# A two-layer mLSTM block and a sparse-attention block on one core: the reciprocal-root chains at the changes of stage, with one SBUF tensor per instruction

## The chip, the cores and the metric

The kernel runs on one core of a Trainium2 chip. The metric is the time of one execution on the device in microseconds (us). Five engines work side by side, each through its own list of instructions in order: TensorE (PE, matmuls and transposes), VectorE (DVE), ScalarE (ACT), GpSimd (POOL) and SyncE (SP, which only issues transfers here). They wait for each other through semaphores. SBUF is the large on-chip memory, PSUM the small one into which TensorE writes its results (the kernel's pool divides it into eight banks).

## The reference, cut to what matters

512 tokens of width 1024 pass through two layers of a first block and one layer of a second. Each layer of the first block is

```python
h = rms_norm(x, g_pre_mix) * (1 + sc_mix) + sh_mix
y = mixer(h, ...)                                   # mLSTM heads and a convolution branch, then @ w_out
x = x + gt_mix * rms_norm(y, g_post_mix)
h = rms_norm(x, g_pre_mlp) * (1 + sc_mlp) + sh_mlp
f = jnp.square(jax.nn.relu(h @ w_ff1)) @ w_ff2
x = x + gt_mlp * rms_norm(f, g_post_mlp)
```

with `rms_norm(x, g) = x * lax.rsqrt(mean(x*x) + 1e-6) * g` per token. The second block has attention, a feed-forward part of the same kind and a last rms_norm. So between two large products there is always this: a sum of squares per token, a reciprocal root, `x` updated, again a sum of squares, again a reciprocal root, and the normed tokens are what the next product reads.

## The kernel before, in words

Every matrix product is done in three matmuls on halves of fp32 numbers (`mm3`, L202 to L204: high by high, high by low, low by high). Weights come as 128x1024 tiles `wr` on SyncE's queue; `prep` makes the high half `w` on ACT (L178) and the low half either on POOL in four pieces of 128x256 (L182) or on DVE in one piece (L69). Which engine it is, is set per chunk of weights by the tuple `pool` of the stage's table `TUNE`. All DVE work that goes through the wrapper `Paced` has line L69, the line of the wrapper, whatever it does; such instructions are told apart by their tiles: `c` are the tiny columns (128x1, 128x2 or 128x4), `E` the token tiles (128x1024), `hT` the transposed and split activations, `t` scratch, `p` PSUM banks.

A change of stage is the place where one product's output, token by token, becomes the next product's input. There are six: after the mixer of layer 0 (near 430 us), after its feed-forward part (near 810), after the mixer of layer 1 (near 1195), after its feed-forward part (near 1575), inside the second block (near 1965), and the last norm at the end. The first four go through `post_norm`. There a tile of 128 tokens is `y[i]`, four tiles in all. When the second half of a tile's product is complete, `ready` lets ACT sum its squares (tile `j`, L580) and POOL multiply it by the gate row (L582). `update` then runs, for a pair of tiles (`w` = 2; first, third and fourth change) or for a single tile (`w` = 1; second change, where `TUNE` has pt=1):

- `s1`, the sum of the two half sums (DVE);
- a reciprocal-root chain `rsqrt` on the 128xw column: a guess from the bits and two polynomial steps, each instruction reading the one before it (DVE, 9 instructions for w > 1, 7 for w = 1);
- `x += r * y` per tile (DVE, tile `E<-E,c,E`, 128x1024), its squares summed on ACT (L593), and a store;
- `norm_T`: a second chain of the same kind, then `x` scaled by its result into `to`. For a pair ACT does both halves of the first tile (L460) and DVE both halves of the second.

After that `norm_T2` transposes on TensorE (L475, 16 transposes of 128x128 for a pair, eight column blocks of two tiles), ACT and DVE bring them out with scale and shift (`t`), ACT writes the high half and DVE the low half of `hT`, and the next product (`p<-hT,w`) can begin with these two tiles while the other two are still on their way.

The order of instructions on each engine is not the order of the source. A scheduler of the tile layer places them by priorities and its own cost estimates. `self.soon()` raises the priority of the norm by `TUNE`'s `bp` (1000, 1000, 200 and 0 in the four changes of stage), `work_off` says where in the stream of matmuls the transposes are emitted. So an edit of the chain's instructions can move others.

The functions of the diff and their callers follow, with the profile's line numbers.

Of the kernel before, what the change touches and what calls it, by code (L numbers as in the profile page):

```python
# [10 lines left out]
I32 = mybir.dt.int32  # L11
AFTER = mybir.DependencyInfo(mybir.DependencyClass.NoSync, mybir.DependencyReason.DATA)
AF = mybir.ActivationFunctionType
OP = mybir.AluOpType

T, D, DFF = 512, 1024, 4096
NL, NH, DH = 2, 4, 256
KC, KM = 31, 4
EPS = 1e-6
# [27 lines left out]
RSQRT_C, RSQRT_GUESS = 1.5 ** 0.2, 0x5f05a21f  # L47
# [25 lines left out]
class Kern:  # L73
    def __init__(self, ctx, tc, A, out, dump=None, stop=None):
        self.tc, self.nc, self.A, self.out = tc, tc.nc, A, out
        self.V = Paced(self, tc.nc.vector)
        self.pt = self.dt = 0.0
# [96 lines left out]
    def prep(self, i):  # L174
        raw, w = self.units[i], self.plan[i][1]
        u = self.units[i] = self.tile("w", (128, 2, 1024), F32R)
        with self.later("prep"):
# [5 lines left out]
            else:  # L183
                self.V.tensor_tensor(u[:, 1, :w], raw[:, :w], f32(u[:, 0, :w]), op=OP.subtract)
        self.prepped += 1
# [36 lines left out]
            nc.scalar.activation(hi, src, AF.Copy if isinstance(scale, float) else AF.Identity, scale=scale)  # L222
            self.V.scalar_tensor_tensor(lo, src, scale, f32(hi), op0=OP.mult, op1=OP.subtract)

    def rsqrt(self, src, w, mul, add, tag=None):

        V = self.V
        vh, z, q, y1, y = (self.c(w, tag) for _ in range(5))

        def half_square(z):  # L230
            a = self.c(w, tag)
            if w == 1:
                V.scalar_tensor_tensor(a, z, vh, z, op0=OP.mult, op1=OP.mult)
            else:
                V.tensor_tensor(a, z, z, op=OP.mult)
                V.tensor_tensor(a, a, vh, op=OP.mult)
            return a
        V.tensor_scalar(vh, src, 0.5 * mul, 0.5 * add, op0=OP.mult, op1=OP.add)
        V.tensor_scalar(z.bitcast(I32), vh.bitcast(I32), -0.5, RSQRT_GUESS, op0=OP.mult, op1=OP.add)
        h = half_square(z)  # L240
        V.scalar_tensor_tensor(q, h, -RSQRT_C ** 2 * 5 / 3, h, op0=OP.add, op1=OP.mult)
        V.scalar_tensor_tensor(y1, q, RSQRT_C ** 4 * 5 / 4, z, op0=OP.add, op1=OP.mult)
        a = half_square(y1)
        V.scalar_tensor_tensor(y, a, 1.5, y1, op0=OP.subtract, op1=OP.mult, reverse0=True)
        return y
# [199 lines left out]
        for ev, b in zip(evacs, bs):  # L445
            ev(b)

    def norm_T(self, ii, xs, ss, G, sh, to):

        V, w = self.V, len(xs)  # L450
        if ii == 0:
            self.new_hT()
        r = self.rsqrt(ss, w, 1.0 / D, EPS)
        for b in range(2):
            h = slice(512 * b, 512 * b + 512)
            for t in range(w):
                if (t if w > 1 else b):
                    V.tensor_scalar(to[t][:, h], xs[t][:, h], r[:, t:t + 1], None, op0=OP.mult)
                else:
                    self.nc.scalar.activation(to[t][:, h], xs[t][:, h], AF.Copy, scale=r[:, t:t + 1])  # L460
        self.xn += to
        if len(self.xn) == 2:
            i, x, self.xn = ii + w - 2, self.xn, []
            for q in range(4):
                self.pend.append((i, lambda q=q: self.norm_T2(i, q, x, G, sh)))
# [92 lines left out]
    def post_norm(self, l, which, nxt):  # L558

        nc, V = self.nc, self.V  # L560
        self.ada_wait(l, range(16 + 24 * which, 24 + 24 * which))
        row = self.gate_row(l, which)
        GS = nxt()
        self.n += 1
        dst = self.dram.tile([T, D], F32, name=f"xd{self.n}")
        src = self.xsrc
        self.xsrc = [dst[i * 128:(i + 1) * 128, :] for i in range(4)]
        xs, ss, w = [None] * 4, {}, 1 if self.tune["pt"] else 2

        def ready(i, nh):  # L570
            y, t = self.y[i], i % w
            self.calm = nh == 1 and CALM
            h = slice(nh * 512, (nh + 1) * 512)
            if nh == 0:
                xs[i] = self.tile("E", (128, D))
                nc.sync.dma_start(xs[i], src[i])
                if t == 0:
                    ss[i // w] = self.c(2 * w)
            with self.soon():
                nc.scalar.activation(self.tile("j", (128, 512), BF16), y[:, h], AF.Square,  # L580
                                     accum_out=ss[i // w][:, w * nh + t:w * nh + t + 1])
                nc.gpsimd.tensor_tensor(y[:, h], y[:, h], row[:, h], op=OP.mult)  # L582
            return (lambda: update(i - t)) if nh and t == w - 1 else None

        def update(i):
            with self.soon():
                s, s1, s2 = ss[i // w], self.c(w), self.c(w)
                V.tensor_tensor(s1, s[:, 0:w], s[:, w:2 * w], op=OP.add)
                r = self.rsqrt(s1, w, 1.0 / D, EPS)
                for t in range(w):  # L590
                    n, x = i + t, xs[i + t]
                    V.scalar_tensor_tensor(x, self.y[n], r[:, t:t + 1], x, op0=OP.mult, op1=OP.add)
                    nc.scalar.activation(self.y[n].bitcast(BF16)[:, 0:D], x, AF.Square, accum_out=s2[:, t:t + 1])  # L593
                    nc.sync.dma_start(self.xsrc[n], x)
                    self.dbg(f"x{l}{which}_{n}", x)
                self.norm_T(i, xs[i:i + w], s2, *GS, self.y[i:i + w])
        return ready


# [1059 lines left out]
```

## Time and profile before

| | |
|---|---|
| median of 3 runs | 2338.77 us (2337.93 to 2339.65) |
| the profiled execution's own time | 2338.5 us |
| its span in the trace | 2336.8 us |
| TensorE busy | 2224.5 us, 95% of the span |
| VectorE / ScalarE / GpSimd busy | 1484.2 / 972.6 / 709.3 us (64% / 42% / 30%) |
| chain that ended last, by engine | PE 75%, DVE 14%, ACT 4%, issue 2%, POOL 2%, DMA 1% |
| mean granted TensorE clock | 0.982 of full speed |

The profile covers one execution. Of TensorE it says that it is nearly always busy; the rest of the span, 112 us, is spread over many short waits. The profile's own time lies 1.7 us above the span, and that part is taken as constant. The chain of work that ended last is followed back from the last instruction, so a share of DVE in it is time in which TensorE had to wait for work on DVE, or in which DVE alone was left at the end.

### The profile page before, as it was taken

The numbers are of one execution on the slowest core, as the hardware profiler recorded it, in microseconds if no ns is written. First come the engines' busy times: TensorE is split into PE (matmuls) and PEld (weight loads), VectorE is DVE, ScalarE is ACT, GpSimd is POOL, SyncE is SP. The second block draws the span as 40 slices with busy tenths as digits, with TensorE's granted clock in tenths as the row PEclk, the third lists the DMA queues.
The fourth block names the chain that finished last, engine by engine and source line by source line (L and its number), as shares of the span: only waits on it lengthen the run. The fifth ranks groups of instructions, "written<-read, shape, count | busy, mean of one in ns | idle before, by whom it ended". The sixth has DMA issues, their size and how long they took to land.

```text
span 2336.8 us, 28930 instructions
## 1 busy us (share of the span) xinstructions
PE 2224.5 (95%) x10552; PEld 1811.9 (78%) x10552; DVE 1484.2 (64%) x2927; ACT 972.6 (42%) x1697; POOL 709.3 (30%) x934
## 2 busy tenths in 40 slices
PE   5998999799999999999989999998989999999998
PEld 3777887688888777788768888877878888888886
DVE  6698998645677669999663233346996435443434
ACT  3435554433232354555443323234447544332322
POOL 4645561425335254565341201212212330000000
PEclk9999999899999999999999999999999999999999
DMA  7524236336666433222333423323111234322232
GB/s 281 166 83 136 64 92 214 109 127 213 211 207 207 145 100 89 74 69 68 114 107 90 135 90 99 99 81 114 55 55 55 64 108 153 104 95 95 88 105 82
DMA packets 77758, 271.37 MB, mean 116 GB/s; under 512 B 9008, under 2 KB 9776, under 8 KB 77616
## 3 DMA queue, kind: packets, MB, share of 16 engines
q1 hardware_dynamic: 69840, 241.21, 32.1%
q0 software_dynamic: 7776, 28.32, 3.8%
q8 instruction: 83, 1.36, 0.2%
q14 instruction: 59, 0.48, 0.1%
HBM read 256.91 MB, written 12.58 MB: 115 GB/s over the span
## 4 chain that ended last, share of the span: by engine, by line
PE 75%; DVE 14%; ACT 4%; issue 2%; POOL 2%; DMA 1%; SPq 0%; ACTq 0%; DVEq 0%; POOLq 0%
PE p L202 23%; PE p L204 23%; PE p L203 23%; DVE p L839 3%; DVE c L69 3%; DVE E L69 1%; POOL w L182 1%; PE p L475 1%; DMA ad<-in_ada_dram 1%; DVE w L69 1%; DVE s L69 1%; ACT w L178 1%; PE p L621 1%; PE p L1211 1%; DVE hT L69 1%
## 5 line engine op out<-in xcount | busy, mean ns | idle before, releaser
L182 POOL TENSOR_TENSOR w<-wr,w 128x256 fp32r<-128x256 f32 x648 | 493.5, 794 | 722.1 <-ACT w L178 629.4
L178 ACT ACTIVATE w<-wr 128x1024 fp32r<-128x1024 f32 (+1 forms) x353 | 369.2, 1048 | 598.1 <-PE p L204 523.1
L202 PE MATMUL p<-hT,w 128*128 128x512 f32 (+1 forms) x1504 | 577.1, 385 | 15.4 <-ACT hT L214 7.3
L203 PE MATMUL p<-hT,w 128*128 128x512 f32 (+1 forms) x1504 | 573.0, 381 | 9.4 <-POOL hT L218 5.4
L204 PE MATMUL p<-hT,w 128*128 128x512 f32 (+1 forms) x1504 | 573.4, 382 | 1.5 <-POOL w L182 1.5
L202 PE MATMUL p<-w,s 128*128 128x512 f32 (+1 forms) x1152 | 450.8, 391 | 3.5 <-ACT s L214 3.5
L204 PE MATMUL p<-w,s 128*128 128x512 f32 (+1 forms) x1152 | 448.8, 390 | 0.6 <-DVE s L69 0.6
L203 PE MATMUL p<-w,s 128*128 128x512 f32 (+1 forms) x1152 | 448.5, 389 | 0.6 <-DVE w L69 0.6
L69 DVE TENSOR_TENSOR w<-wr,w 128x1024 fp32r<-128x1024 f32 (+1 forms) x187 | 233.0, 1247 | 290.9 <-ACT w L178 290.5
L202 PEld LDWEIGHTS p<-hT,w 128*128 128x128 f32 x1504 | 286.2, 191 | 74.7 <-ACT hT L214 9.6
L839 DVE SCALAR_TENSOR_TENSOR p<-ga,ad,p 128x495 f32<-128x495 f32 (+24 forms) x480 | 339.3, 728 | 6.6 <-ACT p L834 5.5
L203 PEld LDWEIGHTS p<-hT,w 128*128 128x128 f32 x1504 | 286.3, 190 | 67.3 <-POOL hT L218 6.5
L204 PEld LDWEIGHTS p<-hT,w 128*128 128x128 f32 x1504 | 286.1, 190 | 57.8 <-POOL w L182 3.8
L202 PEld LDWEIGHTS p<-w,s 128*128 128x128 f32 x1152 | 217.1, 188 | 52.1 <-ACT s L214 4.5
L204 PEld LDWEIGHTS p<-w,s 128*128 128x128 f32 x1152 | 217.0, 188 | 50.1 <-DVE s L69 1.5
L203 PEld LDWEIGHTS p<-w,s 128*128 128x128 f32 x1152 | 217.3, 189 | 49.3 <-DVE w L69 1.0
L69 DVE TENSOR_TENSOR E<-p,E 128x512 f32<-128x512 f32 (+4 forms) x152 | 94.8, 638 | 145.7 <-PE p L204 117.5
L69 DVE SCALAR_TENSOR_TENSOR t<-p,t 128x512 f32<-128x512 f32 x96 | 65.9, 687 | 127.8 <-ACT t L1033 127.8
L296 DVE SCALAR_TENSOR_TENSOR ad<-ad,ad 128x1024 f32<-128x1024 f32 x80 | 107.2, 1345 | 53.6 <-DMA ad<-in_ada_dram 53.6
L1033 ACT ACTIVATE t<-p 128x512 f32<-128x512 f32 x96 | 56.7, 590 | 163.7 <-PE p L204 163.7
L69 DVE TENSOR_TENSOR s<-t,s 128x512 fp32r<-128x512 f32 (+1 forms) x100 | 102.1, 1021 | 12.8 <-ACT s L1035 7.3
L582 POOL TENSOR_TENSOR E<-E,s 128x512 f32<-128x512 f32 x32 | 45.9, 1441 | 168.7 <-ACT j L580 168.7
(272 smaller groups left out, 2648.7 us busy)
## 6 DMA issues: line engine op xcount, KB each, us to landing
wr<-in_ff_dram SPq DMA_DIRECT2D x128, 512.0 KB, 3.8
wr<-in_win_dram SPq DMA_DIRECT2D x64, 512.0 KB, 3.8
ad<-in_ada_dram POOLq DMA_DIRECT2D x54, 512.0 KB, 4.8
wr<-in_wout_dram SPq DMA_DIRECT2D x40, 512.0 KB, 3.8
wr<-in_up_dram SPq DMA_DIRECT2D x32, 512.0 KB, 3.6
wr<-in_down_dram SPq DMA_DIRECT2D x32, 512.0 KB, 3.5
ad<-in_ada_dram SPq DMA_DIRECT2D x26, 512.0 KB, 4.6
xd<-E SPq DMA_DIRECT2D x20, 512.0 KB, 2.7
```

The costliest lines, as they stand in the source:

```text
L69: return f(out, *a, **kw)
L178: self.nc.scalar.activation(u[:, 0, :w], raw[:, :w], AF.Copy)
L182: self.nc.gpsimd.tensor_tensor(u[:, 1, o:e], raw[:, o:e], f32(u[:, 0, o:e]), op=OP.subtract)
L202: mm(out, lh, rh, start=first, stop=False)
L203: mm(out, lh, rl, start=False, stop=False)
L204: self.mm = mm(out, ll, rh, start=False, stop=last)
L296: return self.nc.vector.scalar_tensor_tensor(w, w, 1.0, self.cact, op0=OP.mult, op1=OP.mult, accum_out=m)
L475: nc.tensor.transpose(p[:, k, 128 * t:128 * t + 128], x[t][:, j * 128:(j + 1) * 128], self.ident)
L582: nc.gpsimd.tensor_tensor(y[:, h], y[:, h], row[:, h], op=OP.mult)
L621: nc.tensor.matmul(p[32 * h:32 * h + 32, (c // 2) * 256:(c // 2) * 256 + 256], wg[:, h, c, e, :], ws[3 * h + c][:, e, :], start=c != 1 and ...
L839: V.scalar_tensor_tensor(y[:, d:], a[:, :T - d], w[:, o - d:o - d + 1], y[:, d:], op0=OP.mult, op1=OP.add)
L1033: nc.scalar.activation(r, p, AF.Relu)
```

## The change

`rsqrt` gets two new forms beside the old one, which stays for 128x4 columns and for the pair chains outside `post_norm`.

- For w = 1, wherever it is called, every instruction becomes a `tensor_scalar`: one tensor, and the other factors as per-partition scalars (pointers to a 128x1 column). There are 7 instructions as before. It serves the second change of stage (eight chains) and the last norm (four chains). `s1` becomes a `tensor_scalar` too.
- For w = 2 with `new` given, three of the intermediate values (`z`, `hp`, `y1`) are written to slots of one PSUM bank (tag `pc`), so that every instruction has at most one tensor in SBUF among its inputs. The square by half is computed as `a = vh*z`, then twice `a*z`, once into PSUM and once into SBUF, since the next step wants both; the chain has 10 instructions in place of 9. It serves the first, third and fourth change of stage (four chains each). The first step, `vh`, still reads SBUF and writes SBUF. The `s1` of a pair still reads two SBUF columns.

```diff
--- before.py
+++ after.py
@@ -222,18 +222,41 @@
             nc.scalar.activation(hi, src, AF.Copy if isinstance(scale, float) else AF.Identity, scale=scale)
             self.V.scalar_tensor_tensor(lo, src, scale, f32(hi), op0=OP.mult, op1=OP.subtract)
 
-    def rsqrt(self, src, w, mul, add, tag=None):
+    def rsqrt(self, src, w, mul, add, tag=None, new=None):
 
         V = self.V
+        if w == 1:
+            vh, z, h, q, y1, a, y = (self.c(w, tag) for _ in range(7))
+            ts = V.tensor_scalar
+            ts(vh, src, -0.5 * mul, -0.5 * add, op0=OP.mult, op1=OP.add)
+            ts(z.bitcast(I32), vh.bitcast(I32), -0.5, RSQRT_GUESS - 2 ** 30, op0=OP.mult, op1=OP.add)
+            ts(h, z, vh, z, op0=OP.mult, op1=OP.mult)
+            ts(q, h, RSQRT_C ** 2 * 5 / 3, h, op0=OP.add, op1=OP.mult)
+            ts(y1, q, RSQRT_C ** 4 * 5 / 4, z, op0=OP.add, op1=OP.mult)
+            ts(a, y1, vh, y1, op0=OP.mult, op1=OP.mult)
+            ts(y, a, 1.5, y1, op0=OP.add, op1=OP.mult)
+            return y
+        if new:
+            vh, a, h, q, b, c, y = (self.c(w, tag) for _ in range(7))
+            z, hp, y1 = (new() for _ in range(3))
+            tt, stt = V.tensor_tensor, V.scalar_tensor_tensor
+            V.tensor_scalar(vh, src, 0.5 * mul, 0.5 * add, op0=OP.mult, op1=OP.add)
+            V.tensor_scalar(z.bitcast(I32), vh.bitcast(I32), -0.5, RSQRT_GUESS, op0=OP.mult, op1=OP.add)
+            tt(a, vh, z, op=OP.mult)
+            tt(hp, a, z, op=OP.mult)
+            tt(h, a, z, op=OP.mult)
+            stt(q, hp, -RSQRT_C ** 2 * 5 / 3, h, op0=OP.add, op1=OP.mult)
+            stt(y1, q, RSQRT_C ** 4 * 5 / 4, z, op0=OP.add, op1=OP.mult)
+            tt(b, vh, y1, op=OP.mult)
+            tt(c, b, y1, op=OP.mult)
+            stt(y, c, 1.5, y1, op0=OP.subtract, op1=OP.mult, reverse0=True)
+            return y
         vh, z, q, y1, y = (self.c(w, tag) for _ in range(5))
 
         def half_square(z):
             a = self.c(w, tag)
-            if w == 1:
-                V.scalar_tensor_tensor(a, z, vh, z, op0=OP.mult, op1=OP.mult)
-            else:
-                V.tensor_tensor(a, z, z, op=OP.mult)
-                V.tensor_tensor(a, a, vh, op=OP.mult)
+            V.tensor_tensor(a, z, z, op=OP.mult)
+            V.tensor_tensor(a, a, vh, op=OP.mult)
             return a
         V.tensor_scalar(vh, src, 0.5 * mul, 0.5 * add, op0=OP.mult, op1=OP.add)
         V.tensor_scalar(z.bitcast(I32), vh.bitcast(I32), -0.5, RSQRT_GUESS, op0=OP.mult, op1=OP.add)
@@ -445,12 +468,12 @@
         for ev, b in zip(evacs, bs):
             ev(b)
 
-    def norm_T(self, ii, xs, ss, G, sh, to):
+    def norm_T(self, ii, xs, ss, G, sh, to, new=None):
 
         V, w = self.V, len(xs)
         if ii == 0:
             self.new_hT()
-        r = self.rsqrt(ss, w, 1.0 / D, EPS)
+        r = self.rsqrt(ss, w, 1.0 / D, EPS, new=new)
         for b in range(2):
             h = slice(512 * b, 512 * b + 512)
             for t in range(w):
@@ -566,6 +589,13 @@
         src = self.xsrc
         self.xsrc = [dst[i * 128:(i + 1) * 128, :] for i in range(4)]
         xs, ss, w = [None] * 4, {}, 1 if self.tune["pt"] else 2
+        scr = []
+
+        def new():
+            if not scr:
+                p = self.bank((128, 64, 8), "pc")
+                scr.extend(p[:, i, 0:w] for i in range(64))
+            return scr.pop()
 
         def ready(i, nh):
             y, t = self.y[i], i % w
@@ -585,15 +615,18 @@
         def update(i):
             with self.soon():
                 s, s1, s2 = ss[i // w], self.c(w), self.c(w)
-                V.tensor_tensor(s1, s[:, 0:w], s[:, w:2 * w], op=OP.add)
-                r = self.rsqrt(s1, w, 1.0 / D, EPS)
+                if w == 1:
+                    V.tensor_scalar(s1, s[:, 0:1], s[:, 1:2], None, op0=OP.add)
+                else:
+                    V.tensor_tensor(s1, s[:, 0:w], s[:, w:2 * w], op=OP.add)
+                r = self.rsqrt(s1, w, 1.0 / D, EPS, new=new)
                 for t in range(w):
                     n, x = i + t, xs[i + t]
                     V.scalar_tensor_tensor(x, self.y[n], r[:, t:t + 1], x, op0=OP.mult, op1=OP.add)
                     nc.scalar.activation(self.y[n].bitcast(BF16)[:, 0:D], x, AF.Square, accum_out=s2[:, t:t + 1])
                     nc.sync.dma_start(self.xsrc[n], x)
                     self.dbg(f"x{l}{which}_{n}", x)
-                self.norm_T(i, xs[i:i + w], s2, *GS, self.y[i:i + w])
+                self.norm_T(i, xs[i:i + w], s2, *GS, self.y[i:i + w], new)
         return ready
```

The scheduler places other instructions differently for this. On TensorE at the first change of stage (line L475 is L498 now; p729 is the accumulator of the last token tile, E579 and E580 are the first pair's normed tiles, hT what the next product reads) the program before has

```order
L204 MATMUL p729_3956<-w730_3957,s714_3897 128x512
L475 MATMUL p759_4135<-identr_82,E579_3181 128x128
...
L475 MATMUL p766_4175<-identr_82,E580_3182 128x128
L202 MATMUL p729_3956<-w730_3957,s715_3903 128x512
L203 MATMUL p729_3956<-w730_3957,s715_3903 128x512
L204 MATMUL p729_3956<-w730_3957,s715_3903 128x512
L202 MATMUL p790_4254<-hT749_4067,w732_3962 128x256
```

and the changed one, in the same place,

```order
L204 MATMUL p729_3956<-w730_3957,s714_3897 128x512
L202 MATMUL p729_3956<-w730_3957,s715_3903 128x512
L203 MATMUL p729_3956<-w730_3957,s715_3903 128x512
L204 MATMUL p729_3956<-w730_3957,s715_3903 128x512
L498 MATMUL p760_4138<-identr_82,E579_3181 128x128
...
L498 MATMUL p767_4178<-identr_82,E580_3182 128x128
L202 MATMUL p791_4259<-hT750_4069,w732_3962 128x256
```

The last three matmuls of the old product stood behind the 16 transposes and now stand ahead of them; it is the same at the third change of stage and at the fourth, where the three had stood between the transposes. At the second, ten matmuls instead of six stand ahead of the first large group of transposes, which are now 12 in a row, and 22 instead of 11 ahead of the last tile's. On VectorE at the fourth change of stage (the first pair's second chain, then what follows; w are weights split for the next product, E1988 or E1990 the evacuation of the last token tile, E1986 or E1988 the DVE half of the pair's normed tiles) the program before has

```order
L69 SCALAR_TENSOR_TENSOR c2259_13344<-c2262_13349 128x2
L69 SCALAR_TENSOR_TENSOR c2260_13345<-c2259_13344,c2258_13343 128x2
L69 TENSOR_TENSOR c2263_13354<-c2260_13345 128x2
L69 TENSOR_TENSOR c2263_13354<-c2263_13354,c2257_13342 128x2
L69 SCALAR_TENSOR_TENSOR c2261_13346<-c2263_13354,c2260_13345 128x2
L69 TENSOR_SCALAR E1986_11402<-E2225_13193,c2261_13346 128x512
L69 TENSOR_TENSOR w2238_13244<-wr2221_13159,w2238_13244 128x1024
L69 TENSOR_TENSOR w2240_13249<-wr2237_13242,w2240_13249 128x1024
...
L69 TENSOR_TENSOR E1988_11404<-p2235_13238,E1988_11404 128x512
```

and the changed one

```order
L69 TENSOR_TENSOR c2262_13356<-c2261_13355,p2257_13335 128x2
L69 TENSOR_TENSOR w2240_13254<-wr2223_13169,w2240_13254 128x1024
L69 TENSOR_TENSOR w2242_13259<-wr2239_13252,w2242_13259 128x1024
L69 SCALAR_TENSOR_TENSOR c2263_13357<-p2257_13335,c2262_13356 128x2
L69 TENSOR_TENSOR E1990_11414<-p2237_13248,E1990_11414 128x512
L69 SCALAR_TENSOR_TENSOR p2257_13335<-c2263_13357,p2257_13335 128x2
L69 TENSOR_TENSOR c2264_13358<-c2260_13354,p2257_13335 128x2
L69 TENSOR_TENSOR c2265_13359<-c2264_13358,p2257_13335 128x2
L69 SCALAR_TENSOR_TENSOR c2266_13360<-c2265_13359,p2257_13335 128x2
...
L69 TENSOR_SCALAR E1988_11412<-E2227_13203,c2266_13360 128x512 x2
```

Two weight splits and the evacuation of the last tile have moved from behind the chain into its middle, and the normed halves come after them all. On ScalarE there the second pair's last sum of squares also moved ahead of the first pair's scaling. On TensorE there the second pair's transposes stand 4 matmuls earlier in the next product than before (after 44 instead of 48, with the remaining ones between and behind them).

## Rows read from the trace of the kernel before

**Rows 1.** The page, part 1: busy us, share of the span, instructions.

```profile
PE 2224.5 (95%) x10552; PEld 1811.9 (78%) x10552; DVE 1484.2 (64%) x2927; ACT 972.6 (42%) x1697; POOL 709.3 (30%) x934
```

**Rows 2.** Waits of TensorE: engine line, releaser: us in total, times, longest.

```profile
PE p L475 <- ACT E L460: 21.7, 7, 4.4
```

**Rows 3.** Timeline of TensorE: start us, us, what; in brackets idle before it, releaser.

```profile
434.87 3.68 PE L475 MATMUL p<-identr,E 128*128 128x128 f32 x16 [3.38 <-ACT E L460]
438.20 0.78 PE L202 MATMUL p<-w,s 128*128 128x512 f32 x1
...
440.24 0.69 PE L202 MATMUL p<-hT,w 128*128 128x256 f32 x2 [0.41 <-ACT hT L214]
...
456.00 0.47 PE L475 MATMUL p<-identr,E 128*128 128x128 f32 x1 [4.42 <-ACT E L460]
...
1221.01 0.47 PE L475 MATMUL p<-identr,E 128*128 128x128 f32 x1 [4.41 <-ACT E L460]
```

**Rows 4.** Timeline of VectorE at the first change of stage.

```profile
429.31 0.38 DVE L69 TENSOR_SCALAR c<-c 128x2 f32<-128x2 f32 x2 [0.62 <-ACT E L593]
...
430.11 1.16 DVE L69 SCALAR_TENSOR_TENSOR c<-c 128x2 f32<-128x2 f32 x1
...
434.03 1.79 DVE L69 TENSOR_SCALAR E<-E,c 128x512 f32<-128x512 f32 x2
...
441.67 1.25 DVE L69 TENSOR_TENSOR c<-c 128x2 f32<-128x2 f32 x1
...
449.32 2.85 DVE L69 SCALAR_TENSOR_TENSOR E<-E,c,E 128x1024 f32<-128x1024 f32 x2
```

**Rows 5.** Timeline of GpSimd, and one row of ScalarE, at the same place.

```profile
429.96 1.29 POOL L582 TENSOR_TENSOR E<-E,s 128x512 f32<-128x512 f32 x1 [6.05 <-ACT j L580]
431.22 5.88 POOL L182 TENSOR_TENSOR w<-wr,w 128x256 fp32r<-128x256 f32 x8
429.79 1.99 ACT L178 ACTIVATE w<-wr 128x1024 fp32r<-128x1024 f32 x2
```

**Rows 6.** Windows: PE, PEld, DVE, ACT, POOL busy (x), PEclk, DMA share, GB/s.

```profile
434.80:438.60 3.80, 3.73 (x17) 3.73 (x18) 2.24 (x5) 1.67 (x5) 2.29 (x3) 0.50 0.59 155
1576.00:1579.40 3.40, 2.89 (x19) 2.21 (x19) 3.40 (x5) 1.85 (x5) 0.00 (x0) 1.00 0.39 95
```

**Rows 7.** VectorE: groups by form, a line's durations (min/median/max), unhindered pair chain.

```profile
L69 DVE TENSOR_SCALAR c<-c 128x1 f32<-128x1 f32 x12 | 1.8, 152 | 4.5 <-ACT E L593 4.4
...
L69 DVE TENSOR_SCALAR c<-c 128x2 f32<-128x2 f32 x1 | 1.2, 1166 | 0.0
...
L839 DVE SCALAR_TENSOR_TENSOR p<-ga,ad,p x480: 691/728/756, 72.5 to 1137.0; 128x508 f32<-128x508 f32 x12, 128x505 f32<-128x505 f32 x11, 128x493 f32<-128x493 f32 x11, 128x490 f32<-128x490 f32 x11
...
1957.99 0.16 DVE L69 TENSOR_TENSOR c<-c 128x2 f32<-128x2 f32 x1 [0.85 <-ACT j L1440]
...
1959.96 0.89 DVE L69 TENSOR_SCALAR ad<-E,c 128x512 f32<-128x512 f32 x2
```

**Rows 8.** Timeline of TensorE and VectorE at the second change of stage.

```profile
812.15 0.33 PE L475 MATMUL p<-identr,E 128*128 128x128 f32 x1 [3.15 <-DVE c L69]
...
832.96 0.33 PE L475 MATMUL p<-identr,E 128*128 128x128 f32 x1 [2.22 <-ACT E L460]
...
808.65 2.49 DVE L69 SCALAR_TENSOR_TENSOR c<-c,c 128x1 f32<-128x1 f32 x3
```

**Rows 9.** Timeline of TensorE and VectorE at the fourth change of stage.

```profile
1576.07 0.33 PE L475 MATMUL p<-identr,E 128*128 128x128 f32 x1 [1.46 <-ACT E L460]
...
1593.75 0.33 PE L475 MATMUL p<-identr,E 128*128 128x128 f32 x1 [2.40 <-ACT E L460]
...
1575.63 2.35 DVE L69 TENSOR_TENSOR w<-wr,w 128x1024 fp32r<-128x1024 f32 x2
...
1581.30 1.28 DVE L69 TENSOR_TENSOR c<-c 128x2 f32<-128x2 f32 x1
```

**Rows 10.** Timeline of VectorE at the last norm (its third step, one pointer scalar).

```profile
2330.72 0.22 DVE L69 SCALAR_TENSOR_TENSOR c<-c,c 128x1 f32<-128x1 f32 x1
```

## The prediction

> **What bounds the kernel now.** I read the page's busy shares first, then TensorE's waits, then the timeline at each change of stage. TensorE is busy for 95% of the span [rows 1], so a shorter instruction elsewhere gains only where TensorE stands and waits for it. The list of waits names such a place: the transposes L475 wait for ScalarE's scaling L460 seven times, 21.7 us in all [rows 2]. At the first change of stage these are 3.38 us before the first pair's transposes and 4.42 us before the second's; the third change repeats them (its 4.41 stands in [rows 3]). ScalarE itself waits there for VectorE's second chain.
>
> Why is that chain late? VectorE starts it at 429.31 and scales with its result at 434.03 [rows 4]: 4.72 us. The same chain with its first sum takes 1957.99 to 1959.96, 1.97 us, inside the second block [rows 7], so one tiny instruction costs 0.2 us. The difference is GpSimd. At 430.11 an instruction on two numbers lasts 1.16 us [rows 4], and it ends with GpSimd's 1.29 us instruction of 429.96; then eight GpSimd pieces run to 437.10 [rows 5] and each chain step takes about one of them. In the same way the second pair's first chain (with the hT conversions between its steps) goes from 441.67 to 449.32 [rows 4].
>
> Which instructions are held? Those with two tensors in SBUF. The convolution taps L839 read one from SBUF and one from PSUM and write PSUM: 480 of them, between 691 and 756 ns [rows 7], never held, although GpSimd works through that stretch. The 128x1 `tensor_scalar` has a mean of 152 ns [rows 7], not held either. These are the two forms that the change uses.
>
> **The pair form, step by step (first and third change).** Ten instructions instead of nine: +0.2 us per chain. That PSUM as output or input costs nothing extra is an assumption; the taps' 756 ns for about 500 elements leaves room for some 0.06 us an instruction, so a chain costs between +0.2 and +0.8 us where nothing held it.
>
> - `vh`, the first step, still reads and writes SBUF. It took 1166 ns once [rows 7], so it stays held where GpSimd is at work when it comes, and I count no gain for it. The Trainium skill says ("SBUF — State Buffer", Who interferes with whom) that a `tensor_scalar` whose tensor and output are both in SBUF may use both ports and then contends with GpSimd as well; the trace agrees with its 1166 ns.
> - First pair. The update chain gets 0.2 us longer. The second chain starts at 429.5, before GpSimd does, and ends at 431.5 in place of 434.03. Now ScalarE is next: two weight conversions keep it until 431.78 [rows 5], 432.0 with the shift. The transposes start 0.84 us behind the chain today [rows 3, 4], so at 432.8 instead of 434.87: 2.1 us.
> - The three matmuls that today follow the transposes run ahead of them and end near 432.2. TensorE's wait shrinks from 3.38 to about 0.6 us. Behind 3.38 us of waiting its granted clock was 0.50, the 1.2 GHz level; behind 1.46 us it was 1.00, 2.4 GHz [rows 6, 9]. So I expect full clock: 16 transposes in 1.9 us instead of 3.68, and the three matmuls, the first of which takes 0.78 us today [rows 3], at full clock too. The next product's first matmul, 5.4 us behind the first transpose today [rows 3], comes some 3.5 us behind, at 436.3 instead of 440.24.
> - Second pair. Its last product is evacuated before, not behind, the first pair's transposes: its `s1` moves from 441.67 to about 435.2. From there today's 7.65 us [rows 4] become about 6.4, shorter by one hold like that of `s1` (1.25 us); the other holds, on the conversions, stay. The two updates start at 441.6 instead of 449.32. Behind them the same work as today, 0.2 us for the tenth step and up to 0.6 us more of holds, since GpSimd's next pieces now fall on them: transposes at 449.1 instead of 456.00, 6.9 us. Is TensorE there by then? Today it takes 11.3 us from 440.24 to the start of its wait, 4.42 us before 456.00; from 436.3 that is 447.6, so the chain still ends last and the 6.9 us count.
>
> First change: -6.9. Third change, the same rows 766 us later and the same moves in the order: -6.9. Bounds for each: -3 (the first pair's gain without clock and move, and 1 us of the second's) and -9 (the second wait also falls so low that the clock stays up).
>
> **The single-tile form (second change).** Seven instructions stay seven, but five have pointer scalars. One pointer made 0.22 us of 0.16 [rows 10]; three steps more have one, and `s1`: +0.25 us per chain. Against that three steps of 2.49 us [rows 8] become about 0.65 in the second tile's second chain, which TensorE waits for 3.15 us [rows 8]. With the hold on the scaling half that is left, the transposes start at about 809.9 instead of 812.15, and four more matmuls (0.9 us at the mean of 0.21 us each, 2224.5 over 10552 [rows 1]) are done by then; the wait falls to about 1 us and the half clock behind it goes (1.2 us). Less 0.5 us for a conversion that TensorE then has to wait for (0.41 in the first change [rows 3]): -4. The last tile's transposes wait 2.22 us today [rows 8]. Eleven more matmuls of half the width now stand ahead of them (1.2 us) and its chain comes 4 to 5 us earlier, so most of that wait and part of the slow clock behind it go: -3. Sum -7; bounds -2 (weights or loads take over) and -9.
>
> **The fourth change** goes the other way. There GpSimd splits no weights, so little is held; instead the scheduler has put two weight splits, 2.35 us together [rows 9], and the last evacuation into the middle of the first pair's second chain, and the scaling comes behind. Then GpSimd's next gate product falls on the scaling as it falls today on `s1`, for 1.28 us [rows 9]. The transposes come at about 1579.6 instead of 1576.07, TensorE waits some 4.3 instead of 1.46 us, and behind such a wait it has run at half clock [rows 3, 6]. The second pair's update starts 1.4 us later; its transposes, today at 1593.75 after 2.40 us of waiting [rows 9], come near 1595.3, but TensorE reaches them only at about 1596.4, with four matmuls still to do. Against today +2.3; bounds 0 and +5.
>
> **The last norm** lies on the path: four pointer steps of 0.06 us, +0.25. The kernel's other chains (128x4 columns, the second block's pair) are unchanged.
>
> **Sum.** -6.9 - 6.9 - 7.0 + 2.3 + 0.25 = -18.2 us. Made against the profiled execution, 2338.5 us, that is 2320.3; the median of the runs is 0.3 us higher. I predict 2321. A measurement of this kernel tells about 0.2% from no change, 4.7 us.
>
> **Rivals.**
>
> - *The next wait takes over.* Each product behind a change needs its weights split in time, and ScalarE and GpSimd work through these splits in the same microseconds [rows 5]. If the second pair still meets its weights or its holds on the four conversions (two SBUF tensors, unchanged), only the first pair's 2 us and 1 to 2 us of clock come through per change: -3 to -4 three times, +2.3 and +0.3, about -8: 2330. For it: all engines are dense there. Against it: no wait for weights is near the length of those on L460.
> - *Reading PSUM is slow.* By this each instruction with PSUM among its inputs is later by some 0.06 us, nothing in a matmul's scale but eight times in a chain, with three chains on the path in each of three changes: about +5, so 2326. Against it: the taps' 691 to 756 ns, PSUM on both sides with a pointer. The Trainium skill gives this rule ("VectorE: DVE Perf Modes", The TRN2 errata): a fixed 120 cycles for PSUM to SBUF against 58 within SBUF. By that figure, an estimate, it is 65 ns an instruction, and the sum would be the same 2326.
> - *The holds do not go.* If an instruction waited for GpSimd whatever it reads, the longer pair chains would pay one more hold of about 0.7 us and only the moved matmuls would gain: within 4 us of before. Against it: 480 taps.
> - *Slower.* The moved weight splits of the fourth change decide: 3.5 us later transposes, half clock over the 40 matmuls behind them as well (4 us at most), and the second pair's wait pushed out with them: +8 there, while the others give -1 each: 2344. It decides from the point where TensorE has no full clock until the second pair's transposes. For it: the order shows the move. Against it: only one of four changes has it, and a wait there of 1.46 us leaves the clock at 1.00 today [rows 6], so it must more than double.
>
> **How the numbers follow.** Forecast, with a range of its own of 2313 to 2325: 0.65. Slow PSUM 0.08, next wait 0.14, holds that stay 0.06, slower 0.07. Faster by over 0.2% takes in the first three, but not quite all of the third: 0.86. Same 0.08, slower 0.06. The range reaches from 2312 to 2333, so it takes in the second and third case and leaves out the last two and the tails.
>
> **What would show it.** Right: tiny DVE instructions of 0.16 to 0.22 us in a row while GpSimd runs; first pair's transposes at the first change about 2 us earlier, without a wait over 1 us and at clock 1.00; second pair's transposes about 7 us earlier; at the second change no wait over 1.5 us; at the fourth a wait of about 4 us before the first pair's transposes. Wrong: chain steps of 0.6 us under GpSimd pieces; a wait for weights in place of L460; the fourth change losing over 5 us.

## The result, and the profile after

The changed kernel takes 2317.0 us (median of 4 runs, 2312.9 to 2324.9) against 2338.4 of the kernel before: ratio 0.9913, 95% interval 0.9899 to 0.9927, or about 20 us less. The forecast was 2321, with 2312 to 2333 as its range. A second timing of it, beside two later versions, gave 2317.3 us and 0.9905 (0.9888 to 0.9921).

The profiled execution was the slowest of the four (2324.9 us; span 2323.2). Against the trace of before it arrives at the first change of stage 7.3 us late, through one long hold in the mixer, on an instruction that the change leaves as it was (last section). So the stages are compared one by one.

TensorE's busy time is what it was [rows 1]; the span is shorter, so what went is waiting. The first part of the page, and the list of TensorE's waits (engine, line, releaser: us in total, times, longest):

```profile
PE 2224.2 (96%) x10552; PEld 1811.2 (78%) x10552; DVE 1477.1 (64%) x2939; ACT 972.4 (42%) x1697; POOL 717.1 (31%) x934
```

```profile
PE p L202 <- ACT hT L214: 10.0, 5, 5.1
PE p L498 <- ACT E L483: 8.8, 6, 2.8
```

L498 and L483 are the old L475 and L460: 21.7 us of waiting for the scaling [rows 2] have become 8.8. L202 rose by 2.3 us: the three matmuls that used to cover a part of that wait now run earlier, and at the first change the wait is 1.52 us (below) where it was 0.41 [rows 3].

Where the time went can be read by laying the two traces side by side: the start of the same matmul (by its place in TensorE's list) in the trace of after minus that in the trace of before, ahead of a change of stage and behind it. The places are the matmuls 1780 and 1990, 3430 and 3640, 5320 and 5520, 6960 and 7250. The difference between the two is what that change of stage gained. "Elsewhere" is the rest up to the last matmul; the last norm's end lies behind that, and its +0.25 is compared in the section on the prediction.

| us | first | second | third | fourth | elsewhere |
|---|---|---|---|---|---|
| predicted | -6.9 | -7.0 | -6.9 | +2.3 | 0 |
| after, first profile | -7.3 | -7.5 | -6.6 | -0.6 | +8.0 |
| after, second profile | -7.5 | -7.8 | -6.1 | -0.6 | +0.6 |

"Elsewhere" moves by several us between executions of one and the same kernel. Where one of the runs below leaves a stage's chains as they were before, the same measure gives -2.2 to +1.5, so a term of 1 to 2 us in the table is within what it moves too.

**First change.** Take the 7.3 us off to compare with [rows 3, 4]. VectorE's second chain of the first pair, and two instructions that are still held:

```profile
430.03 1.17 DVE L69 TENSOR_SCALAR c<-c 128x2 f32<-128x2 f32 x1
...
436.75 0.17 DVE L69 TENSOR_SCALAR c<-c 128x2 f32<-128x2 f32 x1 [0.62 <-ACT E L626]
436.95 0.16 DVE L69 TENSOR_SCALAR p<-c 128x2 int32<-128x2 int32 x1
437.15 0.16 DVE L69 TENSOR_TENSOR c<-c,p 128x2 f32<-128x2 f32 x1
437.34 0.17 DVE L69 TENSOR_TENSOR p<-c,p 128x2 f32<-128x2 f32 x1
...
438.12 0.35 DVE L69 TENSOR_TENSOR c<-c,p 128x2 f32<-128x2 f32 x2
438.50 0.16 DVE L69 SCALAR_TENSOR_TENSOR c<-c,p 128x2 f32<-128x2 f32 x1
...
441.97 0.56 DVE L69 TENSOR_TENSOR c<-c 128x2 f32<-128x2 f32 x1
```

The ten steps take 1.91 us (436.75 to 438.66) where the nine took 4.72, although GpSimd began a gate product at 437.40 and its weight pieces at 438.65. Still held are `vh` of the update chain (1.17 us) and, a little, `s1` (0.56). On TensorE (timeline, then windows with PE, PEld, DVE, ACT and POOL busy, PEclk, DMA share, GB/s):

```profile
439.89 1.97 PE L498 MATMUL p<-identr,E 128*128 128x128 f32 x16 [0.44 <-ACT E L483]
443.38 0.51 PE L202 MATMUL p<-hT,w 128*128 128x256 f32 x2 [1.52 <-ACT hT L214]
...
456.47 1.09 PE L498 MATMUL p<-identr,E 128*128 128x128 f32 x8 [1.92 <-ACT E L483]
458.57 1.97 PE L498 MATMUL p<-identr,E 128*128 128x128 f32 x8 [1.00 <-ACT t L508]
```

```profile
439.80:442.00 2.20, 1.97 (x16) 1.73 (x16) 2.20 (x5) 1.48 (x5) 2.20 (x4) 1.00 0.00 0
...
458.40:460.80 2.40, 2.23 (x11) 2.23 (x11) 1.33 (x3) 1.49 (x4) 0.00 (x0) 0.50 0.21 84
...
1564.70:1569.40 4.70, 3.94 (x16) 3.01 (x16) 4.43 (x10) 4.03 (x8) 0.73 (x1) 0.50 0.32 105
```

Transposes at 439.89 - 7.26 = 432.6 (predicted 432.8), the next product at 436.1 (436.3), the second pair's transposes at 449.2 (449.1). The wait of 3.38 us is 0.44, and 16 transposes take 1.97 us at the granted clock of 1.00 instead of 3.68 at 0.50 [rows 3, 6]. The second pair's wait is 1.92 instead of 4.42, and the last eight transposes fall to 0.50, the 1.2 GHz level, behind that wait and another of 1.00.

**Second change.** Its waits of 3.15 and 2.22 us [rows 8] are 0.18 and 0.97 (0.53 in the second profile); three pointer steps take 0.78 us (predicted 0.65) instead of 2.49:

```profile
808.02 0.78 DVE L69 TENSOR_SCALAR c<-c,c 128x1 f32<-128x1 f32 x3
```

```profile
809.38 1.60 PE L498 MATMUL p<-identr,E 128*128 128x128 f32 x12 [0.18 <-DVE c L69]
...
828.32 0.88 PE L498 MATMUL p<-identr,E 128*128 128x128 f32 x6 [0.97 <-ACT E L483]
```

The two traces are level ahead of this change of stage, so its first large group of transposes comes 2.8 us earlier than the 812.15 of before (predicted 809.9). Up to the last tile's transposes 4.7 us are gained (predicted 4), with them 7.5. How much of this the moved matmuls bring by themselves was not measured: in every run with single tiles and the new form they moved too.

**Fourth change.** TensorE's transposes of the two pairs, and what ScalarE and VectorE do ahead of the first:

```profile
1564.78 0.69 PE L498 MATMUL p<-identr,E 128*128 128x128 f32 x2 [2.81 <-ACT E L483]
1565.77 3.25 PE L498 MATMUL p<-identr,E 128*128 128x128 f32 x14 [0.30 <-DVE E L69]
...
1580.82 1.47 PE L498 MATMUL p<-identr,E 128*128 128x128 f32 x12
...
1564.01 0.72 ACT L483 ACTIVATE E<-E,c 128x512 f32<-128x512 f32 x1
...
1560.24 2.36 DVE L69 TENSOR_TENSOR w<-wr,w 128x1024 fp32r<-128x1024 f32 x2
...
1564.20 1.91 DVE L69 TENSOR_SCALAR E<-E,c 128x512 f32<-128x512 f32 x2
```

The first wait has grown from 1.46 to 2.81 us [rows 9], and TensorE then runs at 0.50 (third window above), as predicted; the second wait of 2.40 us is gone, as it is when TensorE comes later than the tiles (1596.4 against 1595.3 in the prediction).

### The profile page after: what moved, and what is told of

It reads as the page before. It is cut to its first block, busy times and chain, and to the rows that moved or that the text cites. A ratio compares the mean times of both kernels' runs of the same rounds, so it can differ in the third digit from the quotient of the medians.

```text
span 2323.2 us, 28953 instructions
## 1 busy us (share of the span) xinstructions
PE 2224.2 (96%) x10552; PEld 1811.2 (78%) x10552; DVE 1477.1 (64%) x2939; ACT 972.4 (42%) x1697; POOL 717.1 (31%) x934
## 4 chain that ended last, share of the span: by engine, by line
PE 76%; DVE 13%; ACT 5%; issue 2%; POOL 2%; DMA 2%; SPq 0%; ACTq 0%; DVEq 0%; POOLq 0%
PE p L202 23%; PE p L204 23%; PE p L203 23%; DVE p L872 4%; DVE c L69 2%; DVE E L69 1%; POOL w L182 1%; DMA ad<-in_ada_dram 1%; ACT w L178 1%; DVE w L69 1%; PE p L654 1%; PE p L1244 1%; DVE cc L69 1%; DVE hT L69 1%; PE p L1245 1%
## 5 line engine op out<-in xcount | busy, mean ns | idle before, releaser
L182 POOL TENSOR_TENSOR w<-wr,w 128x256 fp32r<-128x256 f32 x648 | 500.8, 806 | 697.6 <-ACT w L178 617.6
L202 PE MATMUL p<-hT,w 128*128 128x512 f32 (+1 forms) x1504 | 578.3, 386 | 17.6 <-ACT hT L214 9.6
L202 PE MATMUL p<-w,s 128*128 128x512 f32 (+1 forms) x1152 | 450.1, 391 | 3.5 <-ACT s L214 3.5
L202 PEld LDWEIGHTS p<-hT,w 128*128 128x128 f32 x1504 | 286.8, 191 | 76.2 <-ACT hT L214 10.8
L202 PEld LDWEIGHTS p<-w,s 128*128 128x128 f32 x1152 | 216.9, 188 | 52.4 <-ACT s L214 4.5
L319 DVE SCALAR_TENSOR_TENSOR ad<-ad,ad 128x1024 f32<-128x1024 f32 x80 | 116.0, 1455 | 53.0 <-DMA ad<-in_ada_dram 52.9
L69 DVE TENSOR_TENSOR s<-t,s 128x512 fp32r<-128x512 f32 (+1 forms) x100 | 96.9, 969 | 11.9 <-ACT s L1068 6.9
```

The lines of the kernel that those rows point to most:

```text
L69: return f(out, *a, **kw)
L182: self.nc.gpsimd.tensor_tensor(u[:, 1, o:e], raw[:, o:e], f32(u[:, 0, o:e]), op=OP.subtract)
L202: mm(out, lh, rh, start=first, stop=False)
L319: return self.nc.vector.scalar_tensor_tensor(w, w, 1.0, self.cact, op0=OP.mult, op1=OP.mult, accum_out=m)
```

## The experiments

All run on the chip with the kernel before beside them. The per-stage numbers are worked out as above, each from its own trace against that of before.

**One form at a time.** The single-tile form alone: the pair branch is switched off.

```diff
-        if new:
+        if new and False:
```

> The single-tile form alone (second change of stage and last norm); pairs keep the old chain. If the terms of the prediction add up and do not lean on each other: -7.0 + 0.25, so 6.7 us under before, ratio 0.997; TensorE's wait of 3.15 us at the second change gone, 3.38 and 4.42 at the first as before. If the gain of one change is given back in the next: under 3 us, ratio above 0.9987.

2331.9 us, ratio 0.9970 (0.9960 to 0.9981): 7 us less, as its term says. By stage: +0.1, -8.2, +1.0, 0.0. TensorE's waits at the first change are the old ones:

```profile
435.51 3.68 PE L498 MATMUL p<-identr,E 128*128 128x128 f32 x16 [3.40 <-ACT E L483]
...
456.67 1.97 PE L498 MATMUL p<-identr,E 128*128 128x128 f32 x8 [4.67 <-ACT E L483]
```

The pair form alone: single tiles run the old seven steps, and their `s1` the old sum.

```diff
-        if w == 1:
+        if w == 1 and False:
```

> The pair form alone (first, third and fourth change); single tiles keep the old chain. By the prediction's terms -6.9 - 6.9 + 2.3 = -11.5 us, ratio 0.9951; by the two traces laid side by side -7.0 - 6.0 - 0.8 = -13.8 us, ratio 0.9941. Together with the single-tile form alone it should make the whole change's 20 us if the terms add.

2326.1 us, ratio 0.9941 (0.9929 to 0.9953), 13.8 us less by the ratio. By stage: -7.7, +0.1, -8.1, +0.9. The two ratios multiply to 0.9911 against 0.9913 measured: within the noise the terms add, and no stage gives back what an earlier one gained.

**The order without the relief.** The prediction's first changes rest on two things at once, chains that are not held and matmuls that the scheduler moved. Here the chain's tensors are in SBUF, and four small copies give the scheduler reason to make the same moves; TensorE's order at the first three changes is then the changed kernel's.

```diff
-            return scr.pop()
+            return scr.pop() if ps else self.c(w)
...
+            u = [new(True) for _ in range(3)]
+            for d in u:
+                V.tensor_copy(d, c)
+            V.tensor_copy(c, d)
             stt(y, c, 1.5, y1, op0=OP.subtract, op1=OP.mult, reverse0=True)
```

> TensorE's and ScalarE's order of the changed kernel at the first three changes of stage, but z, hp and y1 of the pair chain are SBUF columns, so the holds stay; four extra instructions on PSUM (0.8 us per chain) make the scheduler place things so. If the relief from GpSimd's holds is what gains: first and third change gain nothing or lose 1 to 3 us each, the second gains 7, in all 2330 to 2338 (ratio 0.997 to 1.000), and the chain's two-column steps again last 0.65 us under GpSimd's pieces. If the moved matmuls and scalings are what gains: within 4 us of the changed kernel, ratio under 0.9935.

2336.2 us, ratio 0.9988 (0.9979 to 0.9997). By stage: -1.4, -7.1, -0.2, +2.5. The holds are back (VectorE, same chain as above; then the transposes that wait for it):

```profile
431.04 0.38 DVE L69 TENSOR_SCALAR c<-c 128x2 f32<-128x2 f32 x2 [0.62 <-ACT E L630]
431.45 1.56 DVE L69 TENSOR_TENSOR c<-c,c 128x2 f32<-128x2 f32 x3
433.05 1.33 DVE L69 SCALAR_TENSOR_TENSOR c<-c,c 128x2 f32<-128x2 f32 x2
434.41 1.33 DVE L69 TENSOR_TENSOR c<-c,c 128x2 f32<-128x2 f32 x2
435.78 0.56 DVE L69 COPY p<-c 128x2 f32<-128x2 f32 x3
```

```profile
437.98 3.67 PE L502 MATMUL p<-identr,E 128*128 128x128 f32 x16 [4.92 <-ACT E L487]
```

0.65 to 0.67 us a step on two SBUF columns, 0.19 a step for the three copies into PSUM among them. With the moves and without the relief the first and third change gain 0.8 us on average, in place of about 7. The copies' own 0.8 us a chain explain no more than 2.4 of the 6 us between, if three chains lie on the path as the prediction counts. So at these two changes the relief is needed, and the moves alone do little; what the relief would bring without the moves was not run.

**The fourth change left old.**

```diff
+        old = l == 1 and which == 1
...
+                n4 = None if old else new
```

> The changed kernel with the old pair chain at the fourth change of stage only. By the prediction's term (+2.3, bounds 0 and +5) it is 2.3 us faster than the changed kernel: ratio 0.9902 against 0.9913. By the two traces side by side the fourth change gained 0.8 us, so it is 0.8 us slower: ratio 0.9917. In its trace the waits before the transposes there are 1.5 and 2.4 us again, as before.

2317.0 us, ratio 0.9908 (0.9893 to 0.9923), against 0.9913 and 0.9905 with it: the same. By stage: -8.7, -7.9, -8.1, -2.2, with the fourth change's waits of 1.47 and 2.39 us back; but a second kernel with the old chain there stood at +1.5, and the run with the single-tile form alone at 0.0. The seven traces with a PSUM chain there stand at -1.0 to +0.9, none of them near +2.3. So the fourth change is worth nothing within 2 us, either way.

**The forms by themselves.** Behind the end of the changed kernel, ten chains of ten equal instructions, once alone and once beside eight GpSimd pieces.

```diff
+                if busy:
+                    for _ in range(8):
+                        nc.gpsimd.tensor_tensor(o, big, seed, op=M)
...
+                for k in range(n):
+                    y = pc() if ps == 2 and k < n - 1 or ps == 1 and k % 2 == 0 else self.c(4)
+                    f(y[:, 0:w], x[:, 0:w])
```

> The changed kernel with ten small groups behind its end: each a chain of ten equal VectorE instructions on tiny columns, once alone and once beside eight GpSimd pieces of 128x256 (about 5.6 us). Alone, all should take 0.15 to 0.22 us. If only instructions with two tensors in SBUF are held: beside GpSimd, two SBUF columns take about 0.65 us each until the pieces end; one SBUF column and one in PSUM stays at 0.16 to 0.17, whatever the output; tensor_scalar from SBUF to SBUF on two numbers is held too (1.17 in the changed kernel), with PSUM on one side it is not; on one number it stays at 0.15, with two pointers at 0.28. If reading PSUM costs extra, the PSUM forms alone are 0.22 or more instead of 0.16. If everything is held whatever it reads, all forms take 0.65 beside GpSimd.

Each form first alone, then beside GpSimd (timeline of VectorE: start, us for the group; and one row of GpSimd's pieces):

```profile
2313.43 1.92 DVE L1596 TENSOR_TENSOR c<-c,c 128x2 f32<-128x2 f32 x10
2315.98 4.07 DVE L1596 TENSOR_TENSOR c<-c,c 128x2 f32<-128x2 f32 x10
...
2341.91 1.58 DVE L1599 TENSOR_TENSOR p<-p,c 128x2 f32<-128x2 f32 x8
...
2345.00 1.58 DVE L1599 TENSOR_TENSOR p<-p,c 128x2 f32<-128x2 f32 x8
...
2360.62 2.00 DVE L1601 TENSOR_SCALAR c<-c 128x2 f32<-128x2 f32 x10
2363.25 4.09 DVE L1601 TENSOR_SCALAR c<-c 128x2 f32<-128x2 f32 x10
...
2388.85 3.06 DVE L1604 TENSOR_SCALAR c<-c,c 128x1 f32<-128x1 f32 x10
2392.52 3.06 DVE L1604 TENSOR_SCALAR c<-c,c 128x1 f32<-128x1 f32 x10
2399.38 2.51 DVE L1605 SCALAR_TENSOR_TENSOR c<-c,c 128x1 f32<-128x1 f32 x10
2402.50 6.77 DVE L1605 SCALAR_TENSOR_TENSOR c<-c,c 128x1 f32<-128x1 f32 x10
...
2315.91 6.33 POOL L1588 TENSOR_TENSOR t<-t,E 128x256 f32<-128x256 f32 x8 [406.06 <-DVE t L1585]
```

Two SBUF columns: 1.92 becomes 4.07. One in SBUF, one in PSUM: 1.58 and 1.58. `tensor_scalar` on two numbers from SBUF to SBUF: 2.00 becomes 4.09. Two pointers on one number: 3.06 and 3.06. The old single-tile step: 2.51 becomes 6.77. This settles which of these forms are held; `tensor_scalar` from SBUF to SBUF is held on two numbers and not on one. By step (durations of a line: minimum/median/maximum in ns):

```profile
L1596 DVE TENSOR_TENSOR c<-c,c x20: 160/161/671, 2313.4 to 2319.9; 128x2 f32<-128x2 f32 x20
...
L1599 DVE TENSOR_TENSOR p<-p,c x16: 168/168/169, 2341.9 to 2346.4; 128x2 f32<-128x2 f32 x16
...
L1602 DVE TENSOR_SCALAR c<-p x10: 158/159/160, 2370.3 to 2374.5; 128x2 f32<-128x2 f32 x10
...
L1603 DVE TENSOR_SCALAR c<-c x20: 153/153/155, 2379.5 to 2383.7; 128x1 f32<-128x1 f32 x20
L1604 DVE TENSOR_SCALAR c<-c,c x20: 272/273/274, 2388.9 to 2395.3; 128x1 f32<-128x1 f32 x20
```

Reading PSUM costs nothing that shows on these columns (158 to 169 ns against 160 within SBUF). `tensor_scalar` with PSUM on one side is not held at all.

**The last hold taken away.** By the probe `vh` can be freed by writing it to PSUM, if the other tensors change sides.

```diff
-            vh, a, h, q, b, c, y = (self.c(w, tag) for _ in range(7))
-            z, hp, y1 = (new() for _ in range(3))
+            z, h, y1, y = (self.c(w, tag) for _ in range(4))
+            vh, a, hp, q, b, c = (new() for _ in range(6))
```

> The changed kernel with the pair chain turned round: vh goes to PSUM (with a, hp, q, b, c) and z, h, y1 stay in SBUF, so that no step reads and writes SBUF alone; still 10 steps, TensorE's order but for one matmul and ScalarE's as in the changed kernel. If the hold of vh is a matter of both sides in SBUF: the step of 1.17 us becomes 0.16 in the first, third and fourth change, the first pair's transposes come 0.5 to 1 us earlier there, 1 to 3 us in all against the changed kernel: ratio 0.9900 to 0.9909. If vh is held because it comes when GpSimd starts, whatever it writes: 1.17 again and ratio 0.9913.

2317.2 us, ratio 0.9896 (0.9878 to 0.9914). By stage: -10.2, -7.6, -8.5, -1.0. The held step is gone at all three changes (1.17 to 0.17), the first pair's wait at the first change with it, and in this trace the last eight transposes of the first change take 1.09 us, as at full clock, instead of 1.97:

```profile
421.48 0.17 DVE L69 TENSOR_SCALAR p<-c 128x2 f32<-128x2 f32 x1
...
430.74 1.91 PE L498 MATMUL p<-identr,E 128*128 128x128 f32 x16
...
447.00 1.09 PE L498 MATMUL p<-identr,E 128*128 128x128 f32 x8 [1.52 <-ACT E L483]
449.10 1.09 PE L498 MATMUL p<-identr,E 128*128 128x128 f32 x8 [1.00 <-ACT t L508]
```

The same chain with the old one at the fourth change:

> The same chain, but the old one at the fourth change of stage. By the prediction's term for that change 2.3 us faster than with it; by the run that left the fourth change alone there is nothing in it: within 1.5 us of the run with vh in PSUM everywhere, less the hold of 1.0 us that is removed there.

2316.5 us, 0.9898 (0.9881 to 0.9916); by stage -8.1, -7.5, -8.5, +1.5. Nothing in the fourth change once more.

And with pairs at the second change of stage too (`pt=0` in its row of the table):

> The chain with vh in PSUM, and pairs in place of single tiles at the second change of stage too. Four chains instead of eight there, 0.16 us instead of 0.22 a step and less work on VectorE, so the last transposes come up to 2 us earlier; but the first tiles wait for each other's second half, as in the first change, and TensorE then waits up to 2 us more before the first transposes. I take the two as equal: within 3 us of the run with vh in PSUM.

2313.8 us, 0.9895 (0.9876 to 0.9913); by stage -10.2, -5.6, -9.0, -0.9. By the trace single tiles are 2 us better there, though the waits before these transposes are gone.

**Three versions side by side,** the changed kernel and the two candidates unedited:

> The changed kernel once more, beside the two below on one chip. 2317 us, ratio 0.9913; TensorE's waits before the transposes as in its first profile (0.44, 1.92, 2.21 and 2.81 us), and the 4.63 us hold in the mixer of layer 0 not there, since seven other profiles lack it: a span of 2314 to 2317 us.

> vh in PSUM, beside the changed kernel. If the 1.0 us less at each of three changes comes through to TensorE: 2 to 3 us under the run beside it. If the second pair's wait (1.5 instead of 1.9 to 2.2 us) is all that TensorE sees: 0.5 to 1.5 us, not to be told from nothing.

> vh in PSUM and pairs at the second change too, beside the two. Its first trace shows no wait before the transposes at the second change (0.23 and 0.18 us in the changed kernel), so it gains at most 1 us there: 1 to 4 us under the changed kernel, ratio 0.9895 to 0.9908.

2317.3 us, 0.9905 (0.9888 to 0.9921); 2314.4, 0.9892 (0.9876 to 0.9909); 2318.3, 0.9906 (0.9891 to 0.9921). Pairs at the second change are no gain, where 1 to 4 us under the changed kernel had been expected. By stage these three stand at -7.5, -7.8, -6.1, -0.6 (table above); -10.2, -7.9, -9.0, -0.9; and -8.3, -5.3, -9.3, -0.7. The kernel with `vh` in PSUM is 1.7 and 1.3 thousandths below the changed one in its two timings (0.9896 against 0.9913, 0.9892 against 0.9905), 3 to 4 us. The traces say the same: the five with `vh` in PSUM stand at -8.1 to -10.2 at the first change and -8.5 to -9.3 at the third, the four with the chain of the change at -7.3 to -8.7 and -6.1 to -8.1; the means differ by 1.6 us at both. A part of the spread inside each group is the clock of the second pair's last eight transposes. At the third change, where they took 1.97 us (granted clock 0.50), the chain of the change stands at -6.1 and -6.6; where they took 1.09 (1.00), at -8.1 twice, and the chain with `vh` in PSUM at -9.0 to -9.3. TensorE's wait before the second pair was 2.14 and 2.21 us in the first two traces and 1.51 to 1.57 in these five; the two traces left, both with `vh` in PSUM, lie between (1.52 and 1.59 us for the eight, -8.5). At the same clock `vh` in PSUM is thus worth 0.9 to 1.2 us there, about the hold of 1.0 that it removes. All three versions beat the kernel before; that `vh` in PSUM beats the changed one is likely and not shown, since the intervals overlap. The long hold in the mixer was absent from the changed kernel's second profile, as expected, but turned up beside it in the run with `vh` in PSUM (last section).

## Why the prediction was right, and where not

- **The cause** (VectorE's tiny steps are held by GpSimd when they have two tensors in SBUF) holds: the probe shows it form by form, and at the first and third change the order without the relief gained next to nothing. Two SBUF inputs are held whatever the output; of the forms with one SBUF input only `tensor_scalar` from SBUF to SBUF on two numbers is, which is `vh`. The Trainium skill ("SBUF — State Buffer", Who interferes with whom) states the rule, that a VectorE instruction with at most one SBUF input, outside its two-port modes, does not contend with GpSimd; the probe agrees with 0.17 us beside GpSimd and alone.
- **First and third change**, -6.9 each: -7.3 and -6.6, in the second profile -7.5 and -6.1. The walk along the order met the first transposes, the next product and the second transposes of the first change within 0.2 us. That the clock comes back in the first pair, and that `vh` stays held, came out as written.
- **Second change**, -7.0: -7.5 and -7.8. Its two parts, -4 and -3, came as -4.7 and -2.8. The first wait fell to 0.18 us rather than about 1; by the prediction's own terms (3.15 less 2.25 less the 0.9 of the moved matmuls) it should have been nothing, so that sentence was a slip; the -4 (2.25, 0.9 and 1.2 less 0.5) follows without it.
- **Fourth change**, +2.3: -0.6 in both profiles, and nothing within 2 us by the run without it. Here a step failed: "GpSimd's next gate product falls on the scaling". It falls on VectorE's tile alone (1.91 us for its two halves; 0.88 for the second pair's, which nothing held). ScalarE scales the first tile (0.72 us for the half that the transposes wait for, 0.70 for the other while GpSimd is idle), and its result lets the transposes start; TensorE saw 0.30 us of VectorE's hold. So the transposes came at 1578.1 in the time of before (1564.78 plus the 13.3 us gained by then), not 1579.6, the wait was 2.81 and not 4.3 us, and TensorE reached the second pair at 1594.1, not 1596.4, with its normed tiles ready. Of these 2.3 us, 1.5 are already there when the transposes start; for the other 0.8, in the stretch between the two pairs, no run gives a cause.
- **The last norm**, +0.25: from the chain's first step to the end of its last 1.70 us (2316.41 to 2318.11) instead of 1.43 (2330.34 to 2331.77), so +0.27. From the start of the last matmul to the end of the span it is 8.64 us before and in the run with the pair form alone, and 8.90 to 8.92 in the ten traces with the new single-tile form (the probe's, which goes on behind the end, left out).
- **Pointers**: 0.06 us each, as taken: 0.153 us with none and 0.273 with two in the probe, 0.21 with one in the changed kernel's chains (0.220 in the probe's old step).
- **Rivals.** *Reading PSUM is slow* is refuted (158 to 169 ns). The Trainium skill ("VectorE: DVE Perf Modes", The TRN2 errata) gives 120 cycles for PSUM against 58 within SBUF; on two numbers no run here shows that difference. *The holds do not go* is refuted. *The next wait takes over* is true in its place and small in its size: 1.92 and 2.21 us of the second pairs' waits stayed at the first and third change, with 1.00 for the evacuation behind them, but the 6 us ahead of them came through. *Slower* needed the fourth change alone to cost 8. One reason given against it was wrong: the wait of 1.46 us did not have to more than double, for behind 2.81 us the granted clock was 0.50.

The four terms summed to -18.5; in each of the two profiles they make -22.0. Of the 3.5 us between the sums 2.9 are the fourth change.

## What to carry to other kernels

Where GpSimd works beside VectorE, count the SBUF tensors of each small VectorE instruction on the critical chain: on these columns a PSUM operand cost nothing that shows and a per-partition scalar 0.06 us, a second SBUF tensor up to a whole GpSimd instruction (1.16 us beside one of 1.29 [rows 4, 5]). An extra step in a chain is cheap (0.19 us) against a held one (0.65 us). Check with a probe of equal steps, alone and beside GpSimd, before rewriting the chain, and look at its first step too: a `tensor_scalar` from SBUF to SBUF on two numbers is held with a single input.

## What the runs showed that was not expected

- Beside pieces in a row, a chain of ten two-tensor steps loses 2.15 us (4.07 less 1.92), which is five holds of 0.41 to 0.5: every second step slips through. With a pointer as well (0.22 alone, 0.77 at most) ten steps lose 4.26 us: the eight that fall into GpSimd's time are all held.
- Two SBUF inputs are held even when the output is in PSUM (probe, its steps in pairs, first two SBUF inputs, then one):

```profile
2335.73 0.57 DVE L1598 TENSOR_TENSOR p<-c,c 128x2 f32<-128x2 f32 x1
2336.34 0.16 DVE L1598 TENSOR_TENSOR c<-p,c 128x2 f32<-128x2 f32 x1
```

- A hold can outlast the piece that caused it. The changed kernel's first profile has in the mixer of layer 0

```profile
334.22 4.63 DVE L69 TENSOR_TENSOR c<-c,ga 128x4 f32<-128x4 f32 x1
...
331.83 4.22 POOL L218 TENSOR_TENSOR s<-E,s 128x256 fp32r<-128x256 f32 x6
336.02 2.81 POOL L182 TENSOR_TENSOR w<-wr,w 128x256 fp32r<-128x256 f32 x4
```

  one instruction on four numbers held to the end of GpSimd's last piece (338.83), over six or seven of them. In eleven of the thirteen profiles, the one of before among them, the longest of this kind lasts 0.41 to 0.45 us; it was 4.6 in two, the changed kernel's first and the second one with `vh` in PSUM, and TensorE came 7.3 and 6.4 us late to the first change there. It is a part of the scatter between executions. What decides it is open.
